# Queries and keys turned by 32x32 vector transposes and transfers through DRAM, not on the matmul engine

## The chip, the cores and the metric

The kernel runs on one core of a Trainium2 chip. The metric is the time of one execution on the device, in microseconds (us). One execution was also taken by the hardware profiler; its page and its trace are what is quoted here. The engines have the page's names: PE is the matmul engine, PEld its loading of the stationary operand, DVE the vector engine, ACT the scalar engine, POOL the general engine (here mostly an issuer of DMAs), SP the engine that issues the loads of the weights.

## What is computed

Two residual layers on 512 tokens of width 1024, in float32. Each layer normalises its input, projects it with one large matrix, runs three branches on parts of the projection, gates each with a SiLU path of its own, projects the branches back and merges them. Cut from the reference:

```python
for l in range(DEPTH):
    h = rms_norm(x, norm_gain[l])
    proj = jnp.einsum('bld,dn->bln', h, w_in[l])
    (qa, fa_f, fa_b, ia, za, ub, vb, zb, qc, kc, vc, zc,
     g_a, g_b, g_c) = jnp.split(proj, split_at, axis=-1)
    ya = hgrn2_bidirectional(qa, fa_f, fa_b, ia, lower[l])
    ya = rms_norm(ya, hg_norm_gain[l]).reshape(B, L, HG_W) * jax.nn.silu(za)
    yb = spatial_gating(gelu(ub), gelu(vb), ...) * jax.nn.silu(zb)
    qh = apply_rope(rms_norm(qc.reshape(B, L, 8, 64), q_norm_gain[l]), cos, sin)
    kh = apply_rope(rms_norm(kc.reshape(B, L, 2, 64), k_norm_gain[l]), cos, sin)
    yc = window_attention(qh, kh, vh, sink_logits[l]) * jax.nn.silu(zc)
    merged = (sigmoid(g_a) * (ya @ w_branch_a[l]) + sigmoid(g_b) * (yb @ w_branch_b[l])
              + sigmoid(g_c) * (yc @ w_branch_c[l]))
    x = x + merged @ w_out[l]
```

The change touches the third branch. Eight query heads share two key heads of 64 values; queries and keys are normalised per head and rotated; a block of 128 queries sees the block of keys before it, its own and the next one (two blocks at the ends of the sequence); and a learned sink logit joins the softmax.

## The kernel before

**Projections.** Every product with a weight matrix is made of three matmuls, because each operand is split into a rounded high part and the remainder: high x high, low x high, high x low. SP loads a weight tile of 128x1024 (`wr`), ACT rounds it (`wh`, L193), and DVE subtracts to get the low part (`wl`, L194). The activations lie in `hth` and `htl`. There are two shapes of loop: `nat_part` (matmuls at L386) puts tokens on the partitions and is used for queries, keys and values, `t_block` (L433) puts features there and is used for gates, recurrence inputs and the merge. An accumulator `pm` (three buffers) takes 24 matmuls of 128x512 in each.

**Side work.** Everything else (attention, recurrence, spatial gating) is written as Python generators in a list `sides`. After each half of a projection block the code calls `advance(2.6)`, which lets the first two generators of the list run until they have used up 2.6 us of estimated work; a generator that yields `None` gives up its turn until the next call. `flush` runs generators to their end. The order so written is then rearranged by a scheduler within each engine, except for instructions under `pin`, which keep their order. Side work shares five PSUM buffers (`ps`), 22 SBUF tiles of 128x1024 (`m4`) and seven of 128x512 (`t2`).

**Queries and keys.** The four query blocks are projected first in a layer, then two gate projections (`main_t`), then the keys and values in two pairs of blocks, then two more gate projections, then the inputs of the recurrence. `norm_rope` (L559) squares, rotates, sums the squares per head and works out the inverse root (`rstd`, L240 on: 11 small DVE operations; the multiplications of it are at L250). `rope_q` (L579) multiplies a query block by that factor (L583), splits it (L193, L194) into a tile `qn` with high and low parts side by side, and has PE transpose its eight 128x128 pieces with the identity `identr` (L592); ACT takes each four out of PSUM (L593). So a query tile `qt` has high parts on partitions 0 to 63 and low parts on 64 to 127. `rope_k` (L597) does the same for a pair of key blocks (L619, L621). The two tiles of keys hold high and low parts, each twice, so that two matmuls make all four products of the parts.

**Attention.** `attention(qb)` (L635) is one generator for each of the four query blocks. For each head it makes two matmuls (L653, L654), one DVE operation that adds the mask and takes the row maximum (L655), later an exponential on ACT (L665) and a scaling on DVE (L675). Then, for each block of 128 keys, DVE transposes within 32x32 squares (L684, four instructions of 256 columns), and POOL's DMA queue writes the tile to DRAM and reads it back with the squares in their turned places (L686, L687). After `LAG` turns come the matmuls with the values (L696), and a product with the gate (L709). The four generators stand in `sides` together, and odd blocks start `STAGGER` turns later. The first merge follows `flush(att)` (L1029). The recurrence's generators `gla` follow in `sides` as the inputs of two heads are there; their small matmuls have 32 columns (L785 and on), their products on DVE are L843.

Of the kernel before, what the change touches and what calls it, by code (L numbers as in the profile page):

```python
# [21 lines left out]
P = 128  # L22
# [7 lines left out]
NEG = -3.0e38  # L30
# [103 lines left out]
STAGGER, LAG = 2, 6  # L134
N_M4, N_T2, N_PM, N_PS = 22, 7, 3, 5


def build(nc, tc, cp, wp, sb, pp, dp, x, wpk, brow, gainb, pvec, wsp, trig, amask, imask, out):
# [96 lines left out]
    identr = cp.tile([P, P], F32R, name="identr")  # L235
    V.tensor_copy(identr, ident)
# [5 lines left out]
    def rstd(ss, n, scale, order=free):  # L242

        v, y, a = small(n), small(n), small(n)
        order(V.tensor_scalar(v, ss, -0.5 * scale, -0.5 * EPS, ALU.mult, ALU.add))

        magic = float(0x5F3759DF - 0x40400000)
        order(V.tensor_scalar(y.bitcast(I32), v.bitcast(I32), -0.5, magic, ALU.mult, ALU.add))
        for _ in range(3):
            order(V.tensor_tensor(a, y, y, ALU.mult))  # L250
# [187 lines left out]
    sides = []  # L438
    credit = [0.0]
# [46 lines left out]
    def flush(upto=()):  # L486
        while sides and (not upto or any(u in sides for u in upto)):
            step([])
        credit[0] = min(credit[0], 0.0)
# [3 lines left out]
    for l in range(L):  # L493
# [60 lines left out]
        qt = [None] * NT  # L554
# [4 lines left out]
        def norm_rope(src, nh, it, tbs, order=free):  # L559
# [12 lines left out]
            order(V.tensor_tensor(b4[:, :, :, 32:64], s4[:, :, :, 0:32], tS[:, :, :, 32:64], ALU.mult))  # L572
            ss = small(nb * nh)
            V.tensor_reduce(ss, sq[:, :w].rearrange("p (h d) -> p h d", d=64), AX, ALU.add)
            V.tensor_tensor(a[:, :w], a[:, :w], b[:, :w], ALU.add)
            r = rstd(ss, nb * nh, 1.0 / 64)
            return a[:, :w].rearrange("p (h d) -> p h d", d=64), r.unsqueeze(2).broadcast_to((P, nb * nh, 64))

        def rope_q(tb, po):  # L579
            q8, r = norm_rope(po.unsqueeze(1), 8, 0, [tb], pin)  # L580
            yield 3.0
            yield None
            V.tensor_tensor(q8, q8, r, ALU.mult)  # L583
            qn = m4((P, 8, P), F32R)
            split(q8, qn[:, :, 0:64], qn[:, :, 64:128])
            for _ in range(6):
                yield None
            qt[tb] = m4((P, 8, P), F32R)
            for k in range(2):
                pt = ps_side((P, 4, P), F32R)  # L590
                for i in range(4):
                    E.transpose(pt[:, i, :], qn[:, 4 * k + i, :], identr)  # L592
                S.copy(qt[tb][:, 4 * k : 4 * k + 4, :], pt.bitcast(F32))  # L593
            done.add(("q", tb))
            yield 0.5

        def rope_k(pair, po):  # L597

            vt = t2((P, 2, P))
            S.copy(vt, po[:, :, 128:256])  # L600
# [4 lines left out]
            k4, r = norm_rope(po[:, :, 0:128], 2, 2, [2 * pair, 2 * pair + 1])  # L605
            yield 1.5
            yield None
            V.tensor_tensor(k4, k4, r, ALU.mult)
            k8 = k4.unsqueeze(2).broadcast_to((P, 4, 2, 64))
            kn = m4((P, 2, 4, 2, 64), F32R)  # L610
            split(k8, kn[:, 0], kn[:, 1])
            yield None
            yield None
            if not ktt:
                ktt.extend((m4((P, 2, T), F32R), m4((P, 2, T), F32R)))
            for hl in range(2):
                pt = ps_side((P, 4, P), F32R)
                for i in range(4):
                    E.transpose(pt[:, i, :], kn[:, hl, i].rearrange("p a d -> p (a d)"), identr)  # L619
                dst = ktt[hl][:, :, 2 * pair * P : 2 * (pair + 1) * P].rearrange("p h (b t) -> p b h t", b=2)  # L620
                S.copy(dst, pt.bitcast(F32).rearrange("p (b h) t -> p b h t", b=2))  # L621
            done.add(("k", pair))
            yield 0.5

        def begin(g):
            next(g)
            sides.append(g)
# [7 lines left out]
        def attention(qb):  # L635
# [3 lines left out]
            for _ in range(STAGGER * (qb % 2)):  # L639
                yield None  # L640
# [4 lines left out]
            sms, pair, pts = [], [], {}  # L645
            for h in range(8):
                g = h // 4
                if h % 2 == 0:
                    sm2 = m4((P, 2, nk))
                    pair.append(sm2)  # L650
                sms.append(sm2[:, h % 2, :])
# [4 lines left out]
                    sms[h], sp[:, :nk], am[:, off : off + nk], 1.0, NEG, ALU.add, ALU.max, mxs[:, h : h + 1]  # L656
# [7 lines left out]
            for h in range(8):  # L664
                S.activation(sms[h], sms[h], AF.Exp, bias=m[:, h : h + 1], accum_out=dn[:, h : h + 1])  # L665
# [8 lines left out]
            for h in range(8):  # L674
                V.tensor_scalar_mul(sms[h], sms[h], rc[:, h : h + 1])  # L675
            yield 2.0
            yield None

            for kb in range(nkb):
                pt = m4((P, 4, 256))  # L680
                xb = pt.rearrange("p b (h j) -> p b h j", j=32)
                for i in range(4):
                    src = pair[i][:, :, kb * P : (kb + 1) * P].rearrange("p h (b j) -> p h b j", j=32)
                    V.transpose(xb[:, :, 2 * i : 2 * i + 2, :].rearrange("p b h j -> p h b j"), src)  # L684
# [3 lines left out]
                pts[kb] = pt  # L688
                yield 1.7
                yield None  # L690
            for _ in range(LAG):
                yield None
            po = ps_side((P, 4, 4, 32))
            for kb in range(nkb):
                for g in range(2):
# [3 lines left out]
                        pts[kb][:, :, 128 * g : 128 * g + 128],  # L699
                        start=kb == 0,  # L700
                        stop=kb == nkb - 1,
                        tile_position=(0, 64 * g),
                    )
            yield 1.0
# [5 lines left out]
            yield 1.5  # L710
# [318 lines left out]
        flush(att)  # L1029
# [52 lines left out]
def host_arrays(inputs):  # L1082
# [7 lines left out]
    def swap(g):  # L1090
# [34 lines left out]
            [np.where(ki >= qi, 0.0, NEG), np.zeros((P, P)), np.where(ki <= qi, 0.0, NEG)], axis=1  # L1125
# [29 lines left out]
```

## Time and profile before

| | before |
|---|---|
| median of 3 runs | 1103.37 us (1102.17 to 1103.82) |
| the profiled execution | 1103.14 us |
| its span in the trace | 1101.3 us |
| granted clock of PE, mean | 0.997 |
| DMA, mean over the span | 116 GB/s |

The span runs from the first to the last instruction that the profiler recorded; the time of the execution contains a little before and behind it. Busy time is the union of an engine's instructions, and matmuls that overlap in the pipeline are counted once. In a row of the timeline the first number is the start and the second the duration, both in us. In a row of a group of instructions `x64 | 6.4, 244 | 0.0` is the count, the group's busy time in us, the mean of one in ns, and the idle time of the engine just ahead of them. In the waits, `PE ps L653 <- DVE sm L655: 0.4, 1, 0.4` reads: PE's instruction at L653 was released by DVE's at L655, after 0.4 us of waiting in sum, once, 0.4 at most. In the table by windows, a row has the window, its length, and then the busy times of PE, PEld, DVE, ACT and POOL.

### The profile page before, as it was taken

To read this page: it belongs to the slowest core of one execution; us is meant where nothing else is said; L and a number is where in the kernel's file an instruction comes from. 1 tells how busy PE (TensorE), PEld (TensorE's weight loads), DVE (VectorE), ACT (ScalarE), POOL (GpSimd) and SP (SyncE) were. 2 spreads that over 40 slices of the span, in tenths; PEclk is the share of its full clock that TensorE was granted. 3 is DMA by queue.
4 is the path that set the end of the run, shared out by engine and by line. 5 is a ranking of instruction groups with operands and counts; after the bars stand their busy time and mean duration, and the time that the engine had idled before them with its cause. 6 is when DMAs were issued, how large, how long until landed. Compare 5 with 4: busy or idle time off the path is not lost.

```text
span 1101.3 us, 17346 instructions
## 1 busy us (share of the span) xinstructions
PE 1090.9 (99%) x7012; PEld 897.7 (82%) x7012; DVE 699.6 (64%) x1503; ACT 427.3 (39%) x679; POOL 48.8 (4%) x71
## 2 busy tenths in 40 slices
PE   8999999999999999999999999999999999999998
PEld 6788786788888888888888877778888888888886
DVE  5965789967864734444387676898678655444432
ACT  4455574343423423233244646543343233322320
POOL 4010110100000000000000020200000000000000
PEclk8999999999999999999999999999999999999999
DMA  8243653432223233235333364723232213333421
GB/s 302 67 127 108 236 191 132 127 89 63 87 78 87 77 96 99 95 94 191 115 116 120 92 201 152 258 60 115 58 96 78 77 58 97 96 95 96 153 106 48
DMA packets 36672, 127.52 MB, mean 116 GB/s; under 512 B 4336, under 2 KB 4848, under 8 KB 36592
## 3 DMA queue, kind: packets, MB, share of 16 engines
q1 hardware_dynamic: 28656, 100.20, 28.8%
q0 software_dynamic: 6208, 22.02, 5.8%
q10 hardware_dynamic: 1728, 4.20, 1.0%
q8 instruction: 55, 0.90, 0.4%
q14 instruction: 25, 0.20, 0.1%
HBM read 111.19 MB, written 15.20 MB: 115 GB/s over the span
## 4 chain that ended last, share of the span: by engine, by line
PE 96%; DVE 2%; ACT 1%; DMA 1%; issue 0%; POOL 0%; POOLq 0%; ACTq 0%
PE pm L433 63%; PE pm L386 19%; PE pm L421 2%; PE ps L696 1%; PE ps L785 1%; PE ps L875 1%; PE ps L653 1%; PE ps L654 1%; PE ps L240 1%; DMA wr<-in_wpk 1%; PE ps L834 1%; PE ps L865 1%; PE ps L882 1%; PE ps L940 1%; PE ps L316 1%; PE ps L810 1%
## 5 line engine op out<-in xcount | busy, mean ns | idle before, releaser
L193 ACT CAST wh<-wr 128x1024 fp32r<-128x1024 f32 x172 | 180.5, 1053 | 410.4 <-PE pm L433 234.7
L433 PE MATMUL pm<-hth,wh 128*128 128x512 f32 x832 | 330.3, 397 | 0.0
L433 PE MATMUL pm<-hth,wl 128*128 128x512 f32 x832 | 324.7, 390 | 0.0
L433 PE MATMUL pm<-htl,wh 128*128 128x512 f32 x832 | 324.2, 390 | 0.0
L194 DVE TENSOR_TENSOR wl<-wr,wh 128x1024 fp32r<-128x1024 f32 x169 | 205.6, 1220 | 183.8 <-PE pm L433 130.5
L433 PEld LDWEIGHTS pm<-hth,wh 128*128 128x128 f32 x832 | 156.2, 188 | 35.1 <-issue 2.9
L433 PEld LDWEIGHTS pm<-hth,wl 128*128 128x128 f32 x832 | 156.2, 188 | 33.3 <-DVE wl L194 0.2
L433 PEld LDWEIGHTS pm<-htl,wh 128*128 128x128 f32 x832 | 156.3, 188 | 31.0 <-issue 0.5
L433 PE MATMUL pm<-m,wh 128*128 128x512 f32 x384 | 118.9, 391 | 0.0
L433 PEld LDWEIGHTS pm<-m,wh 128*128 128x128 f32 x384 | 71.6, 188 | 14.7
L843 DVE TENSOR_TENSOR m<-m,f 128x512 f32<-128x512 f32 x112 | 74.5, 690 | 10.0 <-PE ps L819 4.0
L386 PE MATMUL pm<-wh,m 128*128 128x512 f32 x256 | 79.1, 389 | 0.0
L386 PE MATMUL pm<-wh,hth 128*128 128x512 f32 x192 | 75.8, 405 | 0.7 <-ACT hth L193 0.7
L386 PE MATMUL pm<-wh,htl 128*128 128x512 f32 x192 | 74.2, 397 | 1.0 <-DVE htl L194 1.0
L433 PE MATMUL pm<-m,wl 128*128 128x512 f32 x192 | 74.8, 389 | 0.0
L386 PE MATMUL pm<-wl,hth 128*128 128x512 f32 x192 | 73.5, 394 | 0.9 <-POOL wl L194 0.9
L386 PEld LDWEIGHTS pm<-wh,m 128*128 128x128 f32 x256 | 48.1, 188 | 9.9
L1019 DVE TENSOR_TENSOR t<-pm,t 128x512 f32<-128x512 f32 x32 | 22.1, 692 | 49.5 <-PE pm L433 49.5
L386 PE MATMUL pm<-wl,m 128*128 128x512 f32 x128 | 49.9, 390 | 0.0
L386 PEld LDWEIGHTS pm<-wh,hth 128*128 128x128 f32 x192 | 36.4, 190 | 11.4 <-issue 2.4
L386 PEld LDWEIGHTS pm<-wl,hth 128*128 128x128 f32 x192 | 36.3, 190 | 9.3 <-POOL wl L194 1.7
L386 PEld LDWEIGHTS pm<-wh,htl 128*128 128x128 f32 x192 | 36.5, 191 | 8.9 <-DVE htl L194 1.9
(168 smaller groups left out, 1246.6 us busy)
## 6 DMA issues: line engine op xcount, KB each, us to landing
wr<-in_wpk SPq DMA_DIRECT2D x172, 512.0 KB, 3.6
pd<-m POOLq DMA_DIRECT2D x20, 512.0 KB, 3.2
m<-pd POOLq DMA_DIRECT2D x20, 512.0 KB, 6.5
m<-in_x SPq DMA_DIRECT2D x8, 512.0 KB, 6.5
x<-m ACTq DMA_DIRECT2D x4, 512.0 KB, 2.6
m<-x SPq DMA_DIRECT2D x4, 512.0 KB, 5.9
out_dram<-m ACTq DMA_DIRECT2D x8, 256.0 KB, 2.0
m<-in_gainb SPq DMA_DIRECT2D x2, 512.0 KB, 6.3
```

Of the source, the lines that this page charges most:

```text
L193: order(S.copy(hi_dst, src))
L194: order(eng.tensor_tensor(lo_dst, src, hi_dst.bitcast(F32), ALU.subtract))
L240: E.matmul(warm[:, :P], ident, ident, start=True, stop=True)
L316: E.transpose(pt[:, k, :], self.xs[tb][:, kk * P : (kk + 1) * P], ident)
L386: E.matmul(po, a, b[:, o : o + 512], start=first and n == 0, stop=last and n == len(passes) - 1)
L421: E.matmul(po[:, k, :], a, b[:, o : o + 256], start=n == 0, stop=n == 23)
L433: E.matmul(po, s, m, start=n == 0, stop=n == 3 * nk - 1)
L653: E.matmul(sp[:, :nk], qt[qb][:, h, :], ktt[0][:, g, k0 * P : k1 * P], start=True, stop=False)
L654: E.matmul(sp[:, :nk], qt[qb][:, h, :], ktt[1][:, g, k0 * P : k1 * P], start=False, stop=True)
L696: E.matmul(po[64 * g : 64 * g + 64], vC[:, k0 + kb, 64 * g : 64 * g + 64], pts[kb][:, :, 128 * g : 128 * g + 128], start=kb == 0, stop=kb ...
L843: V.tensor_tensor(v, v, custom(ff, of, ([sd, 2], [2, ng], [0, m])), ALU.mult)
L1019: V.tensor_tensor(sg, po, sg, ALU.mult)
```

## The change

The eight transposes of each query block and of each pair of key blocks are no longer made by PE. `turn32` does for queries and keys what the kernel already does for the attention weights: a transpose within 32x32 squares on DVE, a write to DRAM, and reads that put the squares in their places. It reads twice, into partitions 0 to 63 and 64 to 127. ACT then rounds the whole turned tile into `qt`, and DVE subtracts on the upper 64 partitions, which leaves the low parts there. The inverse norm of the queries isn't multiplied into them; it is worked out once for the whole layer (`rq`, 32 columns) and goes into the score operation as its scale. The mask's value becomes -1e30 for that.

In the attention the scores of a query block lie in one tile `scores` (one buffer), so a block of keys is turned with one transpose of 1024 columns, not four of 256. The four query blocks run one after the other in one generator, `all_attention`; the products with the values are generators of their own in a second list, `timed`, that is served first and whose turns go by count alone. `LAG` goes from 6 to 8, `QLAG` of 11 turns stands between a read and its use, and `m4` has 19 buffers, not 22.

```diff
@@ advance, flush
+    def run_timed():
+        for g in list(timed):
+            c = 0.0
+            while c is not None:
+                credit[0] -= c
+                c = next(g, "end")
+                if c == "end":
+                    timed.remove(g)
+                    c = None
...
     def advance(us):
         credit[0] += us
         waiting = []
+        run_timed()
         while sides and credit[0] > 0:
...
+        def turn32(src, dst):
+            n = src.shape[1]
+            x = t2((P, 2, n, 32))
+            V.transpose(x.rearrange("p c n j -> p n c j"), src.rearrange("p n (c j) -> p n c j", j=32))
+            xd = dp.tile([P, 2, 32 * n], F32, name=nm("xd"))
+            G.dma_start(xd, x.rearrange("p c n j -> p c (n j)"))
+            for half in range(2):
+                G.dma_start(dst[64 * half : 64 * half + 64], xd.rearrange("(a i) c n -> (i c) a n", i=32))
 
         def rope_q(tb, po):
-            q8, r = norm_rope(po.unsqueeze(1), 8, 0, [tb], pin)
+            if tb == 0:
+                rq.append(rows(8 * NT))
+            q8, sq = rotate(po.unsqueeze(1), 8, 0, [tb], pin)
             yield 3.0
-            V.tensor_tensor(q8, q8, r, ALU.mult)
-            qn = m4((P, 8, P), F32R)
-            split(q8, qn[:, :, 0:64], qn[:, :, 64:128])
...
+            V.tensor_reduce(rq[0][:, 8 * tb : 8 * tb + 8], sq, AX, ALU.add)
+            qr = m4((P, 4, 256))
+            turn32(q8, qr)
+            yield 1.5
+            if tb == NT - 1:
...
+                rq.append(rstd(rq[0], 8 * NT, 1.0 / 64, small=rows))
+            for _ in range(QLAG):
+                yield None
             qt[tb] = m4((P, 8, P), F32R)
-            for k in range(2):
-                pt = ps_side((P, 4, P), F32R)
-                for i in range(4):
-                    E.transpose(pt[:, i, :], qn[:, 4 * k + i, :], identr)
-                S.copy(qt[tb][:, 4 * k : 4 * k + 4, :], pt.bitcast(F32))
+            qv = qr.rearrange("p a (h j) -> p h a j", j=32)
+            qo = qt[tb].rearrange("p h (a j) -> p h a j", j=32)
+            S.copy(qo, qv)
+            V.tensor_tensor(qo[64:], qv[64:], qo[64:].bitcast(F32), ALU.subtract)
...
         def rope_k(pair, po):
...
+            kr = t2((P, 4, P))
+            turn32(k4, kr)
+            yield 1.0
+            for _ in range(QLAG):
+                yield None
...
-            for hl in range(2):
-                pt = ps_side((P, 4, P), F32R)
-                for i in range(4):
-                    E.transpose(pt[:, i, :], kn[:, hl, i].rearrange("p a d -> p (a d)"), identr)
...
+                S.copy(ko[0], kv)
+                V.tensor_tensor(ko[1], kv, ko[0].bitcast(F32), ALU.subtract)
...
         def attention(qb):
...
-            for _ in range(STAGGER * (qb % 2)):
-                yield None
...
                 V.tensor_tensor_reduce(
-                    sms[h], sp[:, :nk], am[:, off : off + nk], 1.0, NEG, ALU.add, ALU.max, mxs[:, h : h + 1]
+                    sm[:, :nkb, h, :], sp[:, :nk].rearrange("p (k t) -> p k t", t=P), amv,
+                    rq[1][:, 8 * qb + h : 8 * qb + h + 1], NEG, ALU.add, ALU.max, mxs[:, h : h + 1],
                 )
...
+                V.transpose(
+                    pt.rearrange("p b (h j) -> p h b j", j=32), sm[:, kb].rearrange("p h (b j) -> p h b j", j=32)
+                )
                 pd = dp.tile([P, 4, 256], F32, name=nm("pd"))
                 G.dma_start(pd, pt)
                 G.dma_start(pt, pd.rearrange("(a j) b n -> (j b) a n", j=32))
...
+            tails.append(values(qb, k0, pts))
+            timed.append(tails[-1])
...
+        def all_attention():
+            for qb in range(NT):
+                yield from attention(qb)
...
-                att = [attention(qb) for qb in range(NT)]
-                sides.extend(att)
+                att, tails = all_attention(), []
+                sides.append(att)
...
-        flush(att)
+        flush([att])
+        flush(tails)
```

How the change moves instructions is shown at three places. The rows give the line, the operation, the output and the inputs with the tile's number, and the shape. First PE in the first layer, between the two gate projections ahead of the keys: `pm_503` and `pm_543` are their accumulators, `m_61_348` is a split query block. Before:

```order
L433 MATMUL pm_503<-hth_125,wh_459 128x512
L433 MATMUL pm_503<-htl_126,wh_459 128x512
L433 MATMUL pm_503<-hth_125,wl_460 128x512
L592 MATMUL ps_531<-identr,m_61_348 128x128 x4
L592 MATMUL ps_537<-identr,m_61_348 128x128 x4
L433 MATMUL pm_543<-hth_125,wh_465 128x512
L433 MATMUL pm_543<-htl_126,wh_465 128x512
```

PE at the same place after the change, where the accumulators are `pm_446` and `pm_481`:

```order
L431 MATMUL pm_446<-hth_123,wh_418 128x512
L431 MATMUL pm_446<-htl_124,wh_418 128x512
L431 MATMUL pm_446<-hth_123,wl_419 128x512
L431 MATMUL pm_481<-hth_123,wh_424 128x512
L431 MATMUL pm_481<-htl_124,wh_424 128x512
```

The eight transposes between the projections are gone, and nothing stands in their place on PE.

Second, PE in the first layer at four of the last query block's scores. Before (`ps_1548` to `ps_1561` are the scores, `pm_1481` and `pm_1572` accumulators of projections):

```order
L433 MATMUL pm_1481<-htl_126,wh_1463 128x512
L433 MATMUL pm_1481<-hth_125,wl_1464 128x512
L653 MATMUL ps_1548<-m_154_885,m_145_831 128x256
L654 MATMUL ps_1548<-m_155_886,m_145_831 128x256
L653 MATMUL ps_1552<-m_154_885,m_145_831 128x256
L654 MATMUL ps_1552<-m_155_886,m_145_831 128x256
L653 MATMUL ps_1557<-m_154_885,m_145_831 128x256
L654 MATMUL ps_1557<-m_155_886,m_145_831 128x256
L653 MATMUL ps_1561<-m_154_885,m_145_831 128x256
L654 MATMUL ps_1561<-m_155_886,m_145_831 128x256
L433 MATMUL pm_1572<-hth_125,wh_1537 128x512
```

PE after the change at the same scores, `ps_2035` to `ps_2047`; `pm_1953` and `pm_2051` are projections:

```order
L431 MATMUL pm_1953<-hth_123,wl_1944 128x512
L687 MATMUL ps_2035<-m_157_910,m_155_881 128x256
L688 MATMUL ps_2035<-m_158_911,m_155_881 128x256
L687 MATMUL ps_2039<-m_157_910,m_155_881 128x256
L688 MATMUL ps_2039<-m_158_911,m_155_881 128x256
L687 MATMUL ps_2043<-m_157_910,m_155_881 128x256
L688 MATMUL ps_2043<-m_158_911,m_155_881 128x256
L687 MATMUL ps_2047<-m_157_910,m_155_881 128x256
L688 MATMUL ps_2047<-m_158_911,m_155_881 128x256
L431 MATMUL pm_2051<-hth_123,wh_2024 128x512
L431 MATMUL pm_2051<-htl_124,wh_2024 128x512
L431 MATMUL pm_2051<-hth_123,wl_2025 128x512
```

These scores now stand later: the same accumulator `pm_1953` has two groups of the recurrence's small matmuls ahead of them, and the next projection, `pm_2051`, has two behind.

Third, DVE after the change at that place: `wl_2025` is the low part of a weight that `pm_2051` needs, `m_315_1828` a gelu of the gating branch, `m_262_1446` and `m_190_1050` tiles of the recurrence, and an `ISA` row with two outputs is a score operation with its row maximum:

```order
L194 TENSOR_TENSOR wl_2025<-wr_1802,wh_2024 128x1024
L951 TENSOR_SCALAR m_315_1828<-m_315_1828 128x512
L689 ISA scores_1910,sm_1907<-ps_2035,am,rows_552 128x2x128
L689 ISA sm_1907 128x1
L952 TENSOR_TENSOR m_315_1828<-pm_1953,m_315_1828 128x512
L689 ISA scores_1910,sm_1907<-ps_2039,am,rows_552 128x2x128
L689 ISA sm_1907 128x1
L689 ISA scores_1910,sm_1907<-ps_2043,am,rows_552 128x2x128
L689 ISA sm_1907 128x1
L954 TENSOR_TENSOR m_315_1828<-pm_1953,m_315_1828 128x512
L689 ISA scores_1910,sm_1907<-ps_2047,am,rows_552 128x2x128
L888 TENSOR_TENSOR m_262_1446<-m_262_1446,f_342_1985 128x2x16x16
```

Score operations, the gating branch and the recurrence alternate on DVE there; before, the last block's scores stood ahead of the recurrence.

More of the change, by code (lines that the diff above doesn't have):

```diff
@@ L240, in build, with rstd @@
         E.matmul(warm[:, :P], ident, ident, start=True, stop=True)
-    def rstd(ss, n, scale, order=free):
+    def rstd(ss, n, scale, order=free, small=small):
         v, y, a = small(n), small(n), small(n)
@@ L486, in flush @@
     def flush(upto=()):
-        while sides and (not upto or any(u in sides for u in upto)):
+        while (sides or timed) and (not upto or any(u in sides + timed for u in upto)):
+            run_timed()
             step([])
@@ L557, in build, with rows, rotate @@
         vC = t2((P, NT, P))
-        def norm_rope(src, nh, it, tbs, order=free):
+        def rows(n):
+            return sb.tile([P, n], F32, name=nm("rows"), tag="rows", bufs=5)
+        def rotate(src, nh, it, tbs, order=free):
             nb = len(tbs)
@@ L604, in rope_k @@
                 G.dma_start(vC[:, 2 * pair + k, :], vd[:, k, :].rearrange("(b j) d -> j b d", j=32))
-            k4, r = norm_rope(po[:, :, 0:128], 2, 2, [2 * pair, 2 * pair + 1])
+            ss = small(4)
+            k4, sq = rotate(po[:, :, 0:128], 2, 2, [2 * pair, 2 * pair + 1])
+            V.tensor_reduce(ss, sq, AX, ALU.add)
+            r = rstd(ss, 4, 1.0 / 64)
             yield 1.5
             yield None
[L608 to L611, printed above, removed]
+            V.tensor_tensor(k4, k4, r.unsqueeze(2).broadcast_to((P, 4, 64)), ALU.mult)
+            kr = t2((P, 4, P))
+            turn32(k4, kr)
+            yield 1.0
+            for _ in range(QLAG):
+                yield None
+            if not ktt:
+                ktt.extend((m4((P, 2, T), F32R), m4((P, 2, T), F32R)))
+            for k in range(2):
+                kv = kr[:, :, 64 * k : 64 * k + 64].rearrange("p a (g j) -> p g a j", j=32)
+                ts = slice((2 * pair + k) * P, (2 * pair + k + 1) * P)
+                ko = [t[:, :, ts].rearrange("p g (a j) -> p g a j", j=32) for t in ktt]
+                S.copy(ko[0], kv)
+                V.tensor_tensor(ko[1], kv, ko[0].bitcast(F32), ALU.subtract)
+            yield 1.0
             yield None
             yield None
-            if not ktt:
-                ktt.extend((m4((P, 2, T), F32R), m4((P, 2, T), F32R)))
-            for hl in range(2):
-                pt = ps_side((P, 4, P), F32R)
-                for i in range(4):
-                    E.transpose(pt[:, i, :], kn[:, hl, i].rearrange("p a d -> p (a d)"), identr)
-                dst = ktt[hl][:, :, 2 * pair * P : 2 * (pair + 1) * P].rearrange("p h (b t) -> p b h t", b=2)
-                S.copy(dst, pt.bitcast(F32).rearrange("p (b h) t -> p b h t", b=2))
             done.add(("k", pair))
-            yield 0.5
         def begin(g):
             next(g)
-            sides.append(g)
+            timed.append(g)
         def do_q(tb, po):
@@ L674, in attention @@
             for h in range(8):
-                V.tensor_scalar_mul(sms[h], sms[h], rc[:, h : h + 1])
-            yield 2.0
+                p = sm[:, :nkb, h, :]
+                V.tensor_scalar_mul(p, p, rc[:, h : h + 1])
+            yield 2.5
             yield None
+            pts = []
             for kb in range(nkb):
                 pt = m4((P, 4, 256))
[L681 to L684, printed above, removed]
+                V.transpose(
+                    pt.rearrange("p b (h j) -> p h b j", j=32), sm[:, kb].rearrange("p h (b j) -> p h b j", j=32)
+                )
                 pd = dp.tile([P, 4, 256], F32, name=nm("pd"))
@@ L693, in attention @@
             po = ps_side((P, 4, 4, 32))
-            for kb in range(nkb):
+            for kb, pt in enumerate(pts):
                 for g in range(2):
@@ L1124, in host_arrays @@
         np.concatenate(
[L1125 removed]
+            [np.where(ki >= qi, 0.0, MASKED), np.zeros((P, P)), np.where(ki <= qi, 0.0, MASKED)], axis=1
         ).astype(np.float32)
```

49 lines of the change are left out of this document (23 added, 26 removed).

## Prediction

> **What bounds the kernel now.** First the page's busy times and its chain of waits, to see which engine carries the end.
>
> ```profile
> span 1101.3 us, 17346 instructions
> PE 1090.9 (99%) x7012; PEld 897.7 (82%) x7012; DVE 699.6 (64%) x1503; ACT 427.3 (39%) x679; POOL 48.8 (4%) x71
> PE 96%; DVE 2%; ACT 1%; DMA 1%; issue 0%; POOL 0%; POOLq 0%; ACTq 0%
> ```
>
> The chain is PE for 96% of its length. The span is 1101.3 us of an execution of 1103.14 us, so 1.84 us lie around it; the median of the runs is 1103.37, 0.23 above this execution. I predict for this execution and do not tell 0.2 us apart. But a busy PE is not a PE at its peak, so the timeline comes next: how far apart do matmuls start, and do they ever wait?
>
> ```profile
> 647.92 0.39 PE L433 MATMUL pm<-hth,wh 128*128 128x512 f32 x1
> ...
> 648.14 0.39 PE L433 MATMUL pm<-htl,wh 128*128 128x512 f32 x1
> ...
> 648.25 1.42 DVE L684 STREAM_TRANSPOSE m<-m 128x256 f32<-128x256 f32 x4
> ```
>
> A projection matmul lasts 0.39 us but the next starts 0.22 us later: they overlap, and what one costs is its step, not its duration. The waits of PE by releaser, and the first window with the quieter ones behind it, tell where PE is not kept fed:
>
> ```profile
> PE ps L316 <- DVE m L306: 1.9, 2, 1.7
> ...
> PE ps L653 <- DVE sm L655: 0.4, 1, 0.4
> ```
>
> ```profile
> 0.00:30.00 30.00, 25.69 (x120) 20.78 (x120) 18.13 (x48) 13.84 (x21) 11.52 (x14) 0.89 0.75 277
> 30.00:60.00 30.00, 28.63 (x154) 24.16 (x154) 28.80 (x84) 14.86 (x23) 0.00 (x0) 1.00 0.30 98
> 60.00:90.00 30.00, 30.00 (x190) 26.47 (x190) 18.56 (x74) 18.01 (x34) 3.45 (x6) 1.00 0.31 97
> ```
>
> (columns: PE, PEld, DVE, ACT, POOL busy with their instructions, granted clock, DMA share, GB/s). The largest of PE's waits is at the normalisation of the first layer's input, which the change leaves; inside the layers one wait of 0.4 us is listed. So the kernel is a string of matmuls laid end to end: a matmul that is taken out shortens it by its step, and a wait that is put in lengthens it.
>
> **What is taken off PE.** The 12 blocks of eight transposes (L592 for queries, L619 for keys) go. Their rows by form, and three of the blocks in the chain:
>
> ```profile
> L592 PE MATMUL ps<-identr,m 128*128 128x128 f32 x64 | 6.4, 244 | 0.0
> ...
> L619 PE MATMUL ps<-identr,m 128*128 128x128 f32 x32 | 3.2, 243 | 0.0
> ```
>
> ```profile
> 49.35 0.64 PE ps L592 x8
> 49.99 2.81 PE pm L433 x12
> ```
>
> ```profile
> 80.19 0.63 PE ps L619 x8
> 80.83 1.23 PE pm L386 x5
> ```
>
> ```profile
> 608.05 5.56 PE pm L433 x24
> 613.62 0.64 PE ps L592 x8
> 614.26 0.75 PE pm L433 x3
> ```
>
> From the first transpose to the next projection matmul a block takes 0.64 us (613.62 to 614.26). 64 + 32 transposes are 12 blocks: 12 x 0.64 = **7.7 us**. That is the whole direct gain, since scores and values products keep their number and shapes. The row's mean, 244 ns, is again a duration with overlap; 96 x 244 ns = 23.4 us would be wrong by the steps just read. The Trainium skill ("TensorE: Matmul & The Clock Gate", Part 4: PE-mode transpose) gives about 275 ns for a transpose in a kernel's context and says that the clock does not engage for it; by that price 96 of them would be 26.4 us and the forecast 1079. Against it stands the 0.64 us for eight, and a granted clock of 1.00 in 60 to 90 us, where four of the blocks lie.
>
> **What comes onto DVE, and what leaves it.** The rows for the operations (mean ns of one is the second number):
>
> ```profile
> L194 DVE TENSOR_TENSOR wl<-wr,wh 128x1024 fp32r<-128x1024 f32 x169 | 205.6, 1220 | 183.8 <-PE pm L433 130.5 <-issue 38.8 <-PE pm L386 9.8
> ...
> L684 DVE STREAM_TRANSPOSE m<-m 128x256 f32<-128x256 f32 x80 | 27.9, 411 | 0.0
> ...
> L655 DVE CUSTOM_DVE_ANT_0 m<-ps,am 128x384 f32<-128x384 f32 x32 | 16.0, 548 | 1.7 <-PE ps L654 1.7
> ...
> L655 DVE CUSTOM_DVE_ANT_0 m<-ps,am 128x256 f32<-128x256 f32 x32 | 11.8, 418 | 5.1 <-PE ps L654 5.1
> ...
> L675 DVE TENSOR_SCALAR m<-m,sm 128x384 f32<-128x384 f32 x32 | 11.0, 417 | 0.1
> ...
> L675 DVE TENSOR_SCALAR m<-m,sm 128x256 f32<-128x256 f32 x32 | 8.9, 349 | 0.1
> L194 DVE TENSOR_TENSOR m<-t,m 128x512 fp32r<-128x512 f32 x12 | 8.2, 689 | 2.5 <-ACT m L193 2.5
> ...
> L583 DVE TENSOR_TENSOR t<-t,sm 128x512 f32<-128x512 f32 x8 | 5.5, 685 | 0.0
> ...
> L655 DVE DVE_READ_ACCUMULATOR2_ANT sm<- 128x1 f32 x64 | 5.3, 83 | 0.0
> ...
> L250 DVE TENSOR_TENSOR sm<-sm 128x8 f32<-128x8 f32 x24 | 3.9, 162 | 0.2
> ```
>
> Per layer, in row durations:
> - Queries lose four products with the factor (685 ns), four splits (689) and four root chains of 11 small operations (11 x 162 = 1.8 us): 12.7 us. They gain four 512-wide transposes, four 64x1024 subtractions and one root chain (1.8, as before, although 32 wide). The trace has a transpose only 256 wide: 411 ns, where a scale of 256 is 349 and a split of 512 is 689. A 512-wide one costs between 0.41 (the 256 row) and 0.82 (two of them); I take 0.69, since the 256 row lies where a half split would. The subtraction has 64 lanes but 1024 columns: 1.22 by the weights' split, at least 0.69. Sum 9.4 us, so -3.3.
> - Keys lose two splits (1.4) and gain two 256-wide transposes and four subtractions of 256 (about 0.42 each): 2.5 us, so +1.1.
> - Attention has 10 transposes of 1024 columns for 40 of 256 (16.4 us). Bounds for one: 0.69 and 4 x 0.41 = 1.64; I take 1.22, the subtraction of that width: -4.2. The scaled score reduction takes its factor from memory and writes with gaps; nothing shows that form. I keep 548 and 418; bounds: a tenth less, and 690 and 550 (a quarter to a third more).
>
> Together -6.4 us a layer of 350. On ACT one 1024-wide copy replaces a cast and two evictions for each query block, which is less work. DVE and ACT end no step of PE now, so none of this is credited.
>
> **Where the cover goes.** Before, four attention generators overlapped and the scores of the last query block (before's L653) were done ahead of the recurrence's small matmuls (L785 on). Now each block follows the one before it, and the first starts later: PE runs 144 projection matmuls between the last key matmul and the first score, 144 x 0.22 = 31.7 us. Into that goes the whole path of a turned key: DVE 0.4, write, read, casts. The DMA rows (KB, us to landing):
>
> ```profile
> pd<-m POOLq DMA_DIRECT2D x20, 512.0 KB, 3.2
> m<-pd POOLq DMA_DIRECT2D x20, 512.0 KB, 6.5
> ...
> vd<-t POOLq DMA_DIRECT2D x4, 128.0 KB, 3.1
> t<-vd POOLq DMA_DIRECT2D x8, 64.0 KB, 2.1
> ```
>
> ```profile
> L687 POOL DMA_DIRECT2D m<-pd x20: 748/766/777, 102.4 to 711.5; - x20
> ...
> DMA to landing us min/median/max: 4.3/6.5/9.8
> ```
>
> (the second answer is that of line L687 alone: ns of an issue, and its reads' landings). 3.1 + 6.5, with two issues of 0.77 and 2 on ACT and DVE, is 13 us: hidden with 18 to spare. A layer's added traffic, 4 x 768 + 2 x 384 KB = 3.8 MB in some 40 us, lifts 98 GB/s to about 190; stages at 239 GB/s (below) kept PE fed.
>
> The price lies later. The third and fourth blocks of queries now fall among the recurrence and the gates, where DVE has least room:
>
> ```profile
> 120.00:160.00 40.00, 40.00 (x186) 31.21 (x183) 29.37 (x83) 23.83 (x53) 5.46 (x8) 1.00 0.69 239
> 160.00:200.00 40.00, 40.00 (x412) 28.95 (x412) 37.57 (x81) 19.37 (x27) 6.97 (x9) 1.00 0.38 132
> 200.00:262.00 62.00, 62.00 (x525) 52.09 (x525) 46.66 (x107) 21.65 (x34) 0.00 (x0) 1.00 0.29 86
> ```
>
> From 160 to 262 us DVE worked 37.57 + 46.66 = 84.2 of 102. The last block's DVE work is 8 x (0.42 + 0.08) + 8 x 0.35 + 2 x 1.22 + 1 of small ones = 10.2 us; of the third block about half its work, scaling and transposes, 8 x 0.42 + 3 x 1.22 = 7.0, moves in; some 4 that stood at 160 (the eight old transposes at 411 ns) go. 84.2 + 13.2 = 97.4, or 95%, and in the first 40 us practically all. DVE takes its instructions in order, and between scores and multiplications stand the splits of weights (1.22 us) that the next projection needs. So PE, which did not wait there, will now meet a split or a score's reduction not yet done. I count two such meetings a layer, each worth about half a split, 0.6 us: 4 x 0.6 = **2.5 us**. Bounds: nothing, if the wide transposes cost 0.69, and 12 us for both layers as worked out under the second rival.
>
> **The sum:** 1103.14 - 7.7 + 2.5 = **1097.9 us**.
>
> **Rivals.**
> 1. *The waits eat the gain.* Score matmuls need one of five side PSUM buffers, while two recurrence heads now hold theirs at the same time. If each of the eight scores of the last block waits for the reduction before it, 8 x 0.42 = 3.4 us a layer: 1103.1 - 7.7 + 6.8 = 1102.2. For it: DVE near full. Against it: in 160 to 200 us DVE was busy for 94% and PE waited nowhere.
> 2. *DVE becomes the bound of that stage: slower.* If the forms that no row shows cost their upper ends, DVE gets in the stage 5 transposes x 0.42, 16 scales x 0.13 (strided, at a split's rate) and 12 reductions x 0.14 = 5.9 us more a layer, and with the room used up all of it lands on PE: 1103.1 - 7.7 + 2.5 + 11.8 = 1109.7. It decides from 5 us a layer on, where 7.7 + 2.2 is spent. Against it: four transposes end in 1.42 us, less than four times the row's mean. The Trainium skill ("TensorE: Matmul & The Clock Gate", What's actually happening) adds that PE falls to half clock after about 3.4 us idle; the trace agrees in its first window alone (0.89), and by that rule each such gap would be followed by 3.4 us of steps at twice 0.22, an estimate of 1.7 us more.
> 3. *Keys and queries arrive late.* If landings take three times the rows, the path is 9.3 + 19.5 + 3.5 = 32 us, some 35 where a write stands behind a read, and PE waits up to 3.3, say 2.5 us a layer: 1103.1 - 7.7 + 5 + 2.5 = 1102.9. For it: writes and reads of one queue (POOL) now stand behind each other. Against it, 18 us to spare and landings of at most 9.8. The Trainium skill ("SBUF — State Buffer", SBUF: two separate sides) warns that DVE operations in a two-port mode keep POOL from writing descriptors. The reads above are issued among DVE's transposes and scales, and the latest took 9.8 us, so the trace shows no such delay.
> 4. *A transpose is worth its duration:* 23.4 us, 1079.7 before waits. The steps speak against it.
>
> **How the numbers follow.** Forecast 0.68 (1095.4 to 1100.9), rival 1 0.16, rival 2 0.08, rival 3 0.05, rival 4 0.03. A measurement tells 0.2%, 2.2 us, from no change. Below 1101.2 are the forecast and rival 4 with a little of the others: faster 0.74. Within 2.2 us rivals 1 and 3: same 0.18. Slower 0.08. The range holds the forecast and rivals 1 and 3: 1095.0 to 1103.0.
>
> **What would show it.** PE: 96 matmuls fewer, projection steps still 0.22 us, DVE sum some 12 us lower. Right: PE's waits list entries of 0.3 to 1.5 us from DVE, all behind the first values product of a layer, and 2 to 3 us in sum. Wrong: none there (1095.4), a wait before the first score (rival 3), waits by the dozen with PE's clock below 1.00 (rival 2), or a transpose row of 1024 columns far from 1.22 us.

## The result, and the profile after

| | before | after |
|---|---|---|
| median | 1103.05 us (1102.17 to 1103.82, 4 runs) | 1094.98 us (1094.94 to 1095.13, 4 runs) |
| span of the profiled execution | 1101.3 us | 1093.2 us |

The ratio is 0.9927, with a 95% interval from 0.991 to 0.9944. The change makes the kernel 8.1 us faster. The forecast was 1097.9, and the time lies 0.02 us below the range's lower end of 1095.0. The sign was right and no rival came true, but the size was 2.9 us short.

The page of the changed kernel, its span, busy times and the engines of the chain:

```profile
span 1093.2 us, 17110 instructions
PE 1081.9 (99%) x6916; PEld 889.5 (81%) x6916; DVE 700.2 (64%) x1384; ACT 422.2 (39%) x661; POOL 70.6 (6%) x107
...
PE 97%; DVE 1%; ACT 1%; issue 0%; POOL 0%; POOLq 0%
```

PE has 7012 - 6916 = 96 matmuls fewer and is still the bound. DVE's sum is the same (699.6 before), where the forecast had it some 12 us lower. The waits of PE in the changed kernel:

```profile
PE ps L314 <- DVE m L304: 3.3, 2, 1.7
PE ps L238 <- POOL ident masks.py:199: 1.3, 1, 1.3
PE pm L384 <- POOL wl L194: 1.0, 1, 1.0
PE ps L830 <- DVE pc L843: 0.5, 2, 0.2
PE pm L384 <- ACT hth L193: 0.5, 2, 0.2
PE pm L384 <- DVE htl L194: 0.5, 1, 0.5
```

Only the fourth is inside a layer; the others are at the kernel's start or at a layer's input. It is at the recurrence, not at a weight's split or a score. So the 2.5 us of meetings between PE and DVE's weight splits aren't there. What DVE's operations came to, by form:

```profile
L719 DVE STREAM_TRANSPOSE m<-scores 128x1024 f32<-128x1024 f32 x20 | 24.4, 1234 | 0.0
...
L689 DVE CUSTOM_DVE_ANT_0 scores<-ps,am,rows 128x384 f32<-128x384 f32 x32 | 17.8, 614 | 0.0
...
L689 DVE CUSTOM_DVE_ANT_0 scores<-ps,am,rows 128x256 f32<-128x256 f32 x32 | 14.2, 479 | 1.7 <-PE ps L688 1.7
L712 DVE TENSOR_SCALAR scores<-scores,sm 128x384 f32<-128x384 f32 x32 | 12.9, 472 | 0.1
...
L712 DVE TENSOR_SCALAR scores<-scores,sm 128x256 f32<-128x256 f32 x32 | 10.1, 387 | 0.1
...
L596 DVE STREAM_TRANSPOSE t<-t 128x512 f32<-128x512 f32 x8 | 5.6, 702 | 0.0
```

The wide transposes cost what was assumed (1.23 and 0.70 us for 1.22 and 0.69). The scores (614 and 479 ns for 548 and 418) and the scales (472 and 387 for 417 and 349) became dearer. And the 80 old transposes had been busy for 27.9 us, not 80 x 411 ns = 32.9, because they overlap: the saving there is 27.9 - 24.4 = 3.5 us, not 8.4.

### The profile page after: what moved, and what is told of

Read it like the earlier page. It is cut to its first block, busy times and chain, and to the rows that moved or that the text cites. A ratio compares the mean times of both kernels' runs of the same rounds, so it can differ in the third digit from the quotient of the medians.

```text
span 1093.2 us, 17110 instructions
## 1 busy us (share of the span) xinstructions
PE 1081.9 (99%) x6916; PEld 889.5 (81%) x6916; DVE 700.2 (64%) x1384; ACT 422.2 (39%) x661; POOL 70.6 (6%) x107
## 4 chain that ended last, share of the span: by engine, by line
PE 97%; DVE 1%; ACT 1%; issue 0%; POOL 0%; POOLq 0%
PE pm L431 64%; PE pm L384 19%; PE pm L419 2%; PE ps L737 2%; PE ps L830 1%; PE ps L920 1%; PE ps L687 1%; PE ps L688 1%; PE ps L238 1%; PE ps L879 1%; PE ps L927 1%; PE ps L910 1%; PE ps L985 1%; PE ps L855 1%; PE ps L314 1%; PE ps L864 0%
```

## Where the time came from, read from the starts of PE's matmuls

Both kernels run the same 4224 projection matmuls. Their order differs at 79 places, in four short stretches, but the n-th has the same shape in both, so it can be laid on the n-th of the other. A group of other matmuls between two of them costs the time between their starts less one step of 0.227 us. First a block of transposes in the timeline of the kernel before:

```profile
613.22 0.40 PE L433 MATMUL pm<-hth,wl 128*128 128x512 f32 x1
613.45 0.81 PE L592 MATMUL ps<-identr,m 128*128 128x128 f32 x8
614.10 0.47 PE L433 MATMUL pm<-hth,wh 128*128 128x512 f32 x1
614.40 0.39 PE L433 MATMUL pm<-htl,wh 128*128 128x512 f32 x1
614.62 0.39 PE L433 MATMUL pm<-hth,wl 128*128 128x512 f32 x1
```

The forecast took the block from its first transpose to the next projection matmul. But the step behind that matmul, 614.10 to 614.40, is 0.30 us and the one after it 0.22 again: switching back costs a further 0.075 us, one matmul late. So a block costs 0.64 + 0.075 = 0.715 us, and twelve cost 8.6 where 7.7 was forecast. (In the one place where scores follow the transposes this second part isn't seen.)

Behind the recurrence's small matmuls it is larger. A whole group of two heads, before:

```profile
191.43 0.39 PE L386 MATMUL pm<-wl,hth 128*128 128x512 f32 x1
191.74 0.76 PE L785 MATMUL ps<-m,t 128*32 128x32 f32 x64
192.44 0.50 PE L433 MATMUL pm<-hth,wh 128*128 128x512 f32 x1
192.77 0.40 PE L433 MATMUL pm<-htl,wh 128*128 128x512 f32 x1
```

And one head's half of such a group, after:

```profile
160.24 0.40 PE L384 MATMUL pm<-wh,hth 128*128 128x512 f32 x1
160.57 0.54 PE L830 MATMUL ps<-m,t 128*32 128x32 f32 x32
161.04 0.50 PE L384 MATMUL pm<-wh,htl 128*128 128x512 f32 x1
```

The whole group costs 192.44 - 191.43 - 0.227 = 0.78 us and 0.11 on the second step. A half costs 0.48 to 0.57 and again 0.11, so two halves are 0.3 to 0.5 us dearer than the whole. The changed kernel has eight such halves, and four pieces of other groups, that the kernel before does not have. Summed over the whole trace:

| us of PE | before | after | change |
|---|---|---|---|
| start of the first projection matmul | 10.08 | 10.50 | +0.4 |
| from there to the 73rd | 28.2 | 27.2 | -1.1 |
| transposes of queries and keys, with the step behind | 8.4 | 0 | -8.4 |
| scores | 20.1 | 19.2 | -0.9 |
| all other groups behind the 73rd, with the step behind | 106.6 | 108.8 | +2.2 |
| the rest | | | -0.4 |
| sum, before rounding | | | -8.1 |

Scores without a wait take 0.353 us a pair of 384 columns and 0.238 of 256 by their starts, in sum 32 x 0.353 + 32 x 0.238 = 18.9 us, so 1.2 us of waits there became 0.3.

## The experiments

The runs are compared with the kernel before on the same chip. Unless told otherwise each is the changed kernel with one edit. "On PE" and a number of us means the n-th projection matmul against that of the changed kernel.

**x_pe: the transposes put back, the rebuilt attention kept.**

```diff
-            turn32(q8, qr)
+            split(q8, qn[:, :, 0:64], qn[:, :, 64:128])
...
-            S.copy(qo, qv)
-            V.tensor_tensor(qo[64:], qv[64:], qo[64:].bitcast(F32), ALU.subtract)
+            for k in range(2):
+                pt = ps_side((P, 4, P), F32R)
+                for i in range(4):
+                    E.transpose(pt[:, i, :], qn[:, 4 * k + i, :], identr)
+                S.copy(qt[tb][:, 4 * k : 4 * k + 4, :], pt.bitcast(F32))
```

(and the same for keys)

> The changed kernel, but queries and keys are split and turned on PE again, in the same places and after the same number of turns; one attention generator, one tile of scores, the factor in the score's scale and the wide transposes stay. Theory A (the gain is the 12 blocks of transposes, and each costs 0.64 us and a further 0.075 us on the second matmul behind it): 1095.0 + 12 x 0.715 = 1103.6 us. Theory B (0.64 us a block, as predicted): 1102.7. Rival (the gain comes from the rebuilt attention): 1095 to 1096.

Measured: 1103.06 us, ratio to before 0.9995 (0.9987 to 1.0004). On PE, 8.46 us are lost between the 73rd matmul and the last, for 8.6 by theory A and 7.7 by B. The transposes account for the whole gain, and everything else that the change does adds up to nothing within the noise: by the table, the gain of the start and of the scores is used up in the recurrence.

**x_att4: the attention as before, queries and keys still through DRAM.**

```diff
-                att, tails = all_attention(), []
-                sides.append(att)
+                att = [attention(qb) for qb in range(NT)]
+                sides.extend(att)
```

(with the four generators, pairs of scores, narrow transposes, LAG 6 and 22 buffers of before)

> The changed kernel, but the attention is that of before: four generators that overlap, scores in pairs, 32x32 transposes of 256 columns; queries and keys still go through DRAM. Theory A (the rebuilt attention costs about 2.3 us in the recurrence by cutting its blocks of small matmuls and by waits there, and saves 0.9 of waits at scores): 1095.0 - 2.3 + 0.9 = 1093.6 us. Rival (one block after the other is what lets the turned queries be ready): waits at the first scores, 1097 or more. If the attention's order does not matter: 1095.

Measured: 1115.21 us, ratio 1.0099 (1.0085 to 1.0112). Theory A was wrong here, and the rival's waits came at another place. Waits of PE, and the window in which the largest falls:

```profile
PE ps L735 <- DMA m<-pd: 8.7, 2, 5.1
PE pm L431 <- DVE m L948: 3.8, 2, 2.1
...
200.00:262.00 62.00, 56.48 (x612) 41.82 (x613) 43.19 (x82) 17.53 (x26) 0.76 (x1) 0.89 0.33 108
```

The values products (L735) stand in PE's queue before their tile is back from DRAM. PE stood for 8.7 us there, both times in the first layer, and its granted clock in that window fell to 0.89: some (1 - 0.89) x 62 = 6.8 us more, by estimate. (The Trainium skill, "TensorE: Matmul & The Clock Gate", What's actually happening, has PE at half clock after about 3.4 us of idling. This window agrees: a mean of 0.89 would be some 14 of its 62 us at half clock, an estimate.) The split of the values into generators with their own count of turns is therefore no mere rewriting: with a later start of the attention, products that follow 6 turns behind are too early.

**x_att4lag9: the same with LAG 9.**

> x_att4 with LAG 9, not 6. In x_att4 PE stood 10.5 us at the last block's values product of the first layer, whose tile was still on its way through DRAM. If that alone made it slow: 1094 to 1096 us. If four overlapping generators are slow of themselves when their queries come late (DVE's order, PSUM): still above 1103.

Measured: 1099.09 us, ratio 0.996 (0.9948 to 0.9972), between the two expectations. Sixteen of the 20 us are gone, and the row of L735 with them. The remaining 4 have their own row:

```profile
PE pm L431 <- DVE m L948: 3.7, 2, 2.0
```

A projection waits for a gelu on DVE (L948) to give its accumulator free. So four overlapping generators are worse than one here, once the queries come late. That DVE's order makes the gelu late is argued, not shown. And the scores don't wait in this run: read as in the table, they take 18.9 us, although four generators overlap.

**x_whole: the small groups kept whole by a fixed order.**

```diff
-                    E.matmul(
+                    pin(E.matmul(
...
+                whole[0] = True
...
+                i = E.matmul(po, s, m, start=n == 0, stop=n == 3 * nk - 1)
+                if whole[0]:
+                    pin(i)
+                    whole[0] = False
```

> The changed kernel, with each group of 32-column matmuls of the recurrence's first levels kept in program order on PE, and the next projection matmul behind it, so that no projection matmul comes between. Theory A (a cut of such a group costs about 0.29 us: 0.18 on its way in and out and 0.108 on the second matmul behind it; some five cuts): 1095.0 - 1.4 = 1093.6 us, with no groups of one head alone. Rival (what is lost there are waits for DVE, and a fixed order adds to them): 1095 to 1098, with more waits at those lines.

Measured: 1105.64 us, ratio 1.0019 (1.0009 to 1.0028). The rival was right, and by more than it said:

```profile
PE ps L837 <- DVE pc L851: 7.1, 6, 3.7
```

The cuts are not carelessness of the order. The second half waits for DVE's selection of the level before (`pc`), and projection matmuls that stand in between cover that wait. 0.3 to 0.5 us for a cut is the cheaper price.

**x_dve and x_dve2: how full is DVE?** Unused maxima on DVE beside the last query block's scores.

```diff
+                if qb == NT - 1:
+                    for _ in range(2):
+                        V.tensor_reduce(idle, am, AX, ALU.max)
```

> The changed kernel, with two maxima over 384 columns (about 0.5 us each, their result is not used) put on DVE behind each of the eight scores of a layer's last query block: some 8.5 us more of DVE a layer in the stage that the prediction called full. If DVE has 5% of room there, as predicted, about 4 us a layer land on PE: 1103 us. If the room is what the trace of the changed kernel shows (89 us busy of 102), nearly all is taken up: 1095 to 1096.5.

Measured: 1109.76 us, ratio 1.0051 (1.0038 to 1.0063), but it tests something else. The maxima needed only the mask, and were done at the start:

```profile
PE ps L315 <- DVE m L305: 9.4, 2, 5.4
PE pm L385 <- DVE htl L194: 7.8, 1, 7.8
```

All 15.7 us on PE are lost by the 145th matmul, and none behind it. The next run reads the score tile, so that the work stays in its stage:

```diff
+                    for _ in range(3):
+                        V.tensor_reduce(idle, sm[:, :nkb, h, :], AX, ALU.max)
```

> The run x_dve did not load the stage in question: its maxima needed nothing but the mask and were done at the kernel's start (15.7 us lost by 60 us). Now three maxima over 256 columns (about 0.37 us each, unused) read the score tile behind each of the last block's eight scores: some 8.9 us a layer. With 5% of DVE free there, as predicted, about 4 us a layer land on PE: 1103 us. With the room that the trace shows (89 of 102 us busy): 1095 to 1096.5.

Measured: 1108.95 us, ratio 1.0042 (1.0029 to 1.0055). Waits of PE, and what was added:

```profile
PE pm L432 <- DVE wl L194: 3.3, 3, 1.9
PE ps L859 <- ACT t L823: 3.0, 1, 3.0
...
L696 DVE TENSOR_REDUCE idle<-scores 128x2 f32<-128x256 f32 x48 | 19.7, 411 | 0.0
...
200.00:262.00 62.00, 58.70 (x436) 46.14 (x435) 50.10 (x108) 27.70 (x50) 6.04 (x9) 0.97 0.44 147
740.00:800.00 60.00, 55.78 (x457) 43.16 (x457) 46.56 (x102) 26.24 (x47) 2.72 (x4) 0.94 0.39 124
```

Of 19.7 / 2 = 9.9 us a layer, 6.8 landed on PE in the first layer and 7.6 in the second. Not all of that is waiting: the granted clock fell to 0.97 and 0.94 in these two windows, where the changed kernel has 1.00, which is worth (1 - 0.97) x 62 = 1.9 and (1 - 0.94) x 60 = 3.6 us, by estimate. Still, the room that the windows of the changed kernel seemed to show is not there:

```profile
160.00:200.00 40.00, 40.00 (x386) 29.95 (x385) 38.50 (x94) 17.49 (x25) 3.91 (x6) 1.00 0.32 107
200.00:262.00 62.00, 62.00 (x468) 50.95 (x467) 50.48 (x112) 30.05 (x54) 6.19 (x9) 1.00 0.45 147
```

DVE worked 89.0 of 102 us, 13 us less than the window, and yet only 2.3 to 3.1 of the 9.9 us did not land on PE; without the lost clock it would be some 5 to 6, by estimate.

**x_dve1: one maximum for each score, not three.**

> x_dve2 with one maximum behind each of the last block's scores, not three: 8 x 0.41 = 3.3 us of DVE a layer instead of 9.9, of which 7.1 and 7.7 us landed on PE. If DVE has a fixed room there of 9.9 - 7.4 = 2.5 us a layer, 0.8 us a layer land: 1095.0 + 1.6 = 1096.6 us. If three quarters of any added work land, however little: 1095.0 + 4.9 = 1099.9. If nothing: 1095.

Measured: 1098.20 us, ratio 0.9956 (0.9944 to 0.9968). Of 3.3 us a layer 2.2 and 1.3 landed, between the two theories. PE's granted clock stayed at 1.00 in the stage, so here the room is plain to read: 1.1 and 2.0 us a layer. PE now waits for weight splits, once in each layer, which the changed kernel doesn't do:

```profile
PE pm L432 <- DVE wl L194: 1.5, 2, 0.8
```

That is the meeting that the forecast described. Its mechanism is real, and it begins just beyond what the change itself loads on DVE.

**x_noscale: less DVE work.** The 64 scalings by the inverse of the sum are left out, so the softmax's weights are no longer normalised.

> The changed kernel without the 64 multiplications that scale the exponentials by the inverse of their sum (left out; 23 us of DVE in both layers). If DVE's load is what cuts the recurrence's groups and delays them (2.3 us in sum): 1093 us. If it is the place of the attention's blocks, whatever DVE has to do: 1095.

Measured: 1094.08 us, ratio 0.9917 (0.9903 to 0.993). 23 us less of DVE bring 0.9. So taking load off DVE is worth little here; some 1.3 of the table's 2.2 us don't hang on how much DVE has to scale.

**x_qlag5 and x_qlag8: an earlier attention.**

```diff
-LAG, QLAG = 8, 11
+LAG, QLAG = 8, 5
```

> The changed kernel with QLAG 5, not 11: the attention starts six turns (some 15 us) earlier. In the order of PE no group of the recurrence's small matmuls is cut any more. Theory A (what the change gives back, about 2.3 us, comes from the last query blocks falling among the recurrence's first levels): 1095.0 - 2.3 = 1092.7 us. Rival (5 turns are too few for write and read, whose landings are 3.6 and 7.9 us in the median): the copies on ACT wait for DMA, the casts of weights behind them are late, and PE waits: 1097 or more. If neither: 1095.

Measured: 1096.32 us (1093.93 to 1100.21), ratio 0.9943 (0.9925 to 0.996). The groups of the recurrence were whole, but the scores waited again:

```profile
PE ps L687 <- DVE sm L689: 0.9, 3, 0.3
```

On PE the profiled execution ends 0.1 us ahead of the changed kernel: what the recurrence got back, the scores took (21.8 us, read as in the table, for 19.2). The median is 1.3 us above the changed kernel's, and the runs spread over 6 us; why isn't shown, since the one with a trace is among the quick ones.

> The changed kernel with QLAG 8, between 11 (as changed) and 5. With 5 the recurrence's groups were whole, but the scores waited for DVE, and the sum was the same. If both prices fall in between: 1094 us. If the two just change places: 1095 to 1096.

Measured: 1094.85 us, ratio 0.9927 (0.9915 to 0.9939): not told from the changed kernel. Whether prices change places isn't settled by it: PE's waits there list none at a score, and one of 0.7 us in sum at the recurrence (L830).

**x_actscale and x_act_q8: the scalings on ACT.**

```diff
-                V.tensor_scalar_mul(p, p, rc[:, h : h + 1])
+                S.activation(p, p, AF.Copy, scale=rc[:, h : h + 1])
```

> The changed kernel with the 64 scalings of the exponentials on ACT, not on DVE (23 us of DVE in both layers). DVE's load below its limit is free by x_noscale, which left the same work out and gained 0.9 us; so 1094.1 us at best. If ACT's queue is what then comes late (its casts of weights stand behind the scalings): 1096 or more.

Measured: 1103.04 us, ratio 0.9999 (0.9989 to 1.001). ACT was late: a scaling takes it 553 ns, the casts of weights wait behind them, and PE for the split:

```profile
PE pm L431 <- DVE wl L194: 5.2, 2, 3.2
...
DVE wl L194 <- ACT wh L193: 3.9, 4, 2.2
```

> Scalings on ACT and QLAG 8 together. If score waits with an earlier start come from DVE alone, moving 23 us off it frees them and the recurrence's groups stay whole: 1093 us. If ACT is then late: 1096 or more.

Measured: 1095.55 us, ratio 0.9935 (0.9923 to 0.9946), no better than the changed kernel. So the price of scalings on ACT hangs on when the attention runs. No version that was run and computes the same beats the change clearly.

**x_start: the start.** In the kernel before, the queries' sum of squares and inverse root are written one turn later.

```diff
-            ss = small(nb * nh)
-            V.tensor_reduce(ss, ...)
...
+            def factor():
+                ss = small(nb * nh)
+                V.tensor_reduce(ss, ...)
+                r = rstd(ss, nb * nh, 1.0 / 64)
```

> The kernel before, with one edit: the sum of squares and the inverse root of queries are written one turn later, behind the rotation, as the change has it for the sum. Theory (in the first layer these small operations stand on DVE between the splits of the layer's input that PE waits for; the runs with the changed order all reach the 73rd projection matmul 26.6 to 27.4 us behind the first, the kernel before 28.2): 27.2 us from the first to the 73rd, and 1103.0 - 1.0 = 1102.0 us if nothing later changes. Rival (that microsecond belongs to this one execution of the kernel before, or to the identity tile): 28.2, and 1103.

Measured: 1104.34 us, ratio 1.0013 (1.0004 to 1.0021), and 29.2 us from the first to the 73rd matmul. Neither number was expected. The scheduler, free to place these operations, put the sum of squares at the old place and the split of the layer's input later. The first such split behind 29 us on DVE, in the kernel before, in the changed one and in x_start:

```profile
32.44 0.68 DVE L194 TENSOR_TENSOR htl<-ps,hth 128x512 fp32r<-128x512 f32 x1
```

```profile
31.59 0.68 DVE L194 TENSOR_TENSOR htl<-ps,hth 128x512 fp32r<-128x512 f32 x1
```

```profile
34.03 0.68 DVE L194 TENSOR_TENSOR htl<-ps,hth 128x512 fp32r<-128x512 f32 x1
```

The three begin 22.4, 21.1 and 23.6 us behind the kernel's first projection matmul, and the 73rd follows after 28.2, 27.2 and 29.2. So in these three traces the start goes with the place of that split: in the kernel before and in x_start, the sum of squares (L574, L577) stands ahead of it on DVE, in the changed kernel behind. What puts it there in the change isn't shown, since this one edit did not bring the microsecond. It isn't the identity tile, since x_pe has one and took 27.4; and it isn't chance of one execution, since the eleven runs with the changed queries whose start nothing else loads took 26.6 to 27.3. The first matmul's own start differs between executions, from 9.8 to 12.2 us, so the +0.4 in the table is no part of the change.

## Why the prediction was off

Two terms of the sum failed. The gain on PE was right in its mechanism and too small by 0.8 us. The price of 2.5 us for PE meeting DVE's late work was not paid: x_pe shows that everything beside the transposes adds up to nothing within the noise (ratio 0.9995).

- **"12 x 0.64 = 7.7 us".** The mechanism was right, and the term was mis-sized. A block costs 0.715 us, since the second projection step behind it is 0.30 and not 0.227. x_pe measured 8.5 us for all twelve, 0.8 more than forecast. The row was in the timeline of before, one line below the one used.
- **The working from steps, not durations.** Right: 23.4 us would have been wrong by 15. By the Trainium skill's 275 ns for a transpose in context ("TensorE: Matmul & The Clock Gate", Part 4: PE-mode transpose) 96 of them would have been 26.4 us, an estimate. The measured 8.5 us are 88 ns for each, in blocks of eight at a granted clock of 1.00.
- **"4 x 0.6 = 2.5 us", PE meeting a split or a score's reduction.** This is the step whose mechanism failed. "PE, which did not wait there, will now meet a split or a score's reduction not yet done": it met none, and "none there (1095.4)" was the prediction's own sign of being wrong. In its place stand 2.2 us in the table, from cuts of the recurrence's groups and the wait for `pc` at L830, against -1.1 at the start and -0.9 at the scores. That 2.2 lies near 2.5 is luck. The load was overestimated: DVE was busy for 89.0 us of 160 to 262, not 97.4, and yet x_dve1 shows that it had only 1.1 to 2.0 us of room. (Two slips in the working change little: 4 x 0.6 is 2.4, and eight transposes at 411 ns are 3.3 us, not "some 4".) The sum of DVE forecast 12 us lower failed on durations that overlap (5 us) and on dearer forms (scores and scales, 32 x 66 + 32 x 61 + 32 x 55 + 32 x 38 ns = 7 us).
- **Nothing credited at the start and at the scores.** "The largest of PE's waits is at the normalisation of the first layer's input, which the change leaves": the wait it leaves, but in its trace the sum of squares no longer stands ahead of the split there, -1.1 us. And the waits at the scores went, -0.9. That is not the serial order's doing: x_att4lag9 has four generators and 18.9 us for its scores, x_qlag5 has the serial order and, with an earlier start, 21.8. By these runs it goes with the later start of the attention. The forecast had looked for waits that the change adds and not for those that it ends.
- **Rival 1, waits at scores:** they became fewer. It was near, all the same: with QLAG 5 they came back.
- **Rival 2, DVE as the bound:** not reached. x_dve2 shows what it would have cost: with 9.9 us a layer, 14.4 in sum. Its point, "from 5 us a layer on", lies at some 6 us a layer in this kernel, an estimate on a straight line: half of the 8.1 us gained is 4.05, between the 1.75 that x_dve1 lost for 3.3 us and the 7.2 of x_dve2 for 9.9.
- **Rival 3, late landings:** not seen. The reads of the turned queries took longer than forecast, 7.9 us in the median:

```profile
m<-xd POOLq DMA_DIRECT2D x16, 256.0 KB, 7.9
xd<-t POOLq DMA_DIRECT2D x8, 256.0 KB, 3.6
```

but PE waited for none, and with six turns less (x_qlag5) for none either.

Sum: 0.8 for the blocks, 1.1 for the start and 0.9 for the scores are 2.8 of the 2.9 us. The start and the scores are read from one trace of each kernel; x_pe bears out only that they and the recurrence cancel.

## What to carry to other kernels

Where matmuls are laid end to end, take a group's price from the starts of the projection matmuls around it and include the second step behind it; a return from a group of another shape costs 0.08 to 0.11 us there, so the number of groups counts beside the number of matmuls. When a change takes work off an engine that others wait for, go through the list of waits of before and ask of each whether it ends. And an engine that is busy for 87% of a stage may have as good as no room: load it a little more and see. When PE does wait, look at its granted clock too: in x_dve2 it made the loss larger than the waits.

## What was not expected of the hardware

- The extra time behind a group shows on the second matmul after it, not on the first: 0.075 us behind eight 128x128 transposes, 0.11 behind 32-column matmuls, 0.41 behind the two matmuls with a tile of ones (their rows' starts in both kernels).
- A scale taken from memory and an output with gaps, which came together, make the score operation 61 to 66 ns dearer, at 256 and 384 columns alike; a scaling whose rows lie apart is 38 to 55 ns dearer.
- Two reads of 256 KB into 64 partitions each landed after 7.9 us in the median, reads of 512 KB into 128 partitions after 5.1 (L724), both on POOL's queue. Whether the partitions or the traffic in their stage does it wasn't tried.
